# Head of a hybrid attention layer: fewer unused products, the second token tile normalised before a copy, and the conditioning rows before its transposes

## The chip, the cores and the metric

The kernel runs on one core of a Trainium2 chip. The metric is the device time of one execution in microseconds, the median over several runs. The engines are TensorE (PE in the profile; PEld its weight loads), VectorE (DVE), ScalarE (ACT), GpSimd (POOL) and SyncE (SP), whose queue issues nearly all loads. Each engine works through its own instructions in order; they wait for each other by semaphores.

## What is computed

One decoder layer in float32: 256 tokens, model width 1024. The part at the start is an adaptive norm, its result feeds one wide input projection, and behind that stand two attention branches, a gated merge and an output projection:

```python
mod = silu(c) @ w_ada + b_ada                       # conditioning: shift, scale, gate
shift, scale, gate = split(mod, 3)
h = rms_norm(x, g_pre) * (1 + scale) + shift        # x: 256 x 1024
proj = h @ w_in                                     # q/kv latents, MoBA q, k, v, gates
...
x = x + gate * rms_norm(y, g_post)
```

`rms_norm` multiplies each token by one over the root of the mean of its squares.

## The kernel before

Tokens lie in two tiles of 128 (`xs[0]`, `xs[1]`). The input comes in two loads: the first tile together with small constants (line 98), then the second tile (line 99). For the projection each weight and each input is split into a rounded part and its remainder, and three products are summed.

The kernel has a head and then a loop. The **head** (lines 309 to 350) makes the transposed, normalised input `xnT`, 8 blocks of 128 columns by 256 tokens. For each tile t: ScalarE squares it and sums (`ss`, line 332); VectorE makes the mean, GpSimd raises it to the power -0.5 (line 337), VectorE scales the tile (`xn[t]`, line 339); TensorE transposes it in two groups of four blocks (`pre_tr(t, 0)` into a bank `acc`, `pre_tr(t, 1)` into a bank `sc`), and a copy brings each group from the bank to `xnT`. The copy is on ScalarE where t equals the group's number and on VectorE otherwise. `pre_tr` records the transposes when it is called and gives back a function that records the copy.

Beside that, the **conditioning**: `ada_rows(j)` has eight products of the conditioning vector (`scp`) with a block of weights that is loaded in two halves (`raw` from `in_wada_dram`); `ada_evac(j)` copies the result to `rws` on ScalarE, `ada_cols(j)` turns it into columns by two narrow products with ones, `ada_ab(j)` makes scale and shift (`ab`) on VectorE. With these ScalarE makes the modulated block `h` of `xnT` (`h_act`), and the first projection product can run.

`busy(n)` (line 316) records n products of a tile of ones with itself; nothing reads them. A float32 product leaves two records in the trace.

The **loop** (`tokens`, with the string `STEP`) runs over the 8 weight blocks: in each step TensorE does the block's products and the next block's conditioning, and ScalarE and VectorE split the next block's weights (`s` and `d`). Raw weights lie in a ring of five buffers; `release` frees one and `pump` issues the next load on the SyncE queue. The first loads are issued in the order of `LOADS`: conditioning block 0 in two halves, weight block 0 in two parts, conditioning 1, weights 1, conditioning 2, and so on.

The order of the work in head and loop is written by hand: `ordered(eng, ...)` makes an instruction follow the last one so recorded on its engine, so program order is engine order there. Only behind the loop does a scheduler set it.

Of the kernel before, what the change touches and what calls it, by code (L numbers as in the profile page):

```python
# [10 lines left out]
FT = mybir.dt.float32  # L11
# [3 lines left out]
OP = mybir.AluOpType  # L15
# [3 lines left out]
P = 128  # L19
D = 1024  # L20
# [42 lines left out]
def hybrid_layer_kernel(ctx: ExitStack, tc: tile.TileContext, x, head, cst, gpost, bgate,  # L63
# [4 lines left out]
    wk = ctx.enter_context(tc.tile_pool(name="wk", bufs=2))  # L68
# [4 lines left out]
    V = nc.vector  # L73
# [4 lines left out]
    def ordered(eng, f, *a, **k):  # L78

        if eng in last_ins:  # L80
            with tc.issue_after(last_ins[eng]):
                r = f(*a, **k)  # L82
        else:
            r = f(*a, **k)
        last_ins[eng] = r.ins
        return r

    def bank(tag):
        return ps.tile([P, 512], FT, name=tag)
# [3 lines left out]
    xs = (first[:, 0:D], first[:, D + HEAD:])  # L93
# [79 lines left out]
    def ada_rows(j):  # L173
        r = raws["ada", j].rearrange("p (k n) -> p k n", k=KT)
        assert got["ada", j] == 2048
        for k in range(KT):
            g = 32 * (k % 4)
            ordered("T", mm, bR[g:g + 32, ROW:ROW + 256], scp[:, k], r[:, k], start=(k < 4), stop=(k >= 4),
                    skip_group_check=True)
        release()  # L180

    def ada_evac(j):
        rws[j] = wk.tile([P, 256], FT, name="rws", tag="acc", bufs=2)
        ordered("A", act, rws[j], bR[:, ROW:ROW + 256], AF.Copy)

    def ada_cols(j):
        r = rws.pop(j)
        for i in range(2):
            ordered("T", mm, bR[:, COL + 8 * i + j:COL + 1 + 8 * i + j], r[:, i * P:(i + 1) * P], ones[:, 0:1],
                    start=False, stop=True, skip_group_check=True)  # L190

    def ada_ab(j):
        ab = hab[j] = wk.tile([P, 2], FT, name="ab", bufs=2)
        ordered("V", V.scalar_tensor_tensor, ab[:, 1:2], bR[:, COL + 8 + j:COL + 9 + j], bsc[:, j:j + 1],
                gpre[:, j:j + 1], op0=OP.add, op1=OP.mult)
        ordered("V", V.tensor_tensor, ab[:, 0:1], bR[:, COL + j:COL + 1 + j], bsh[:, j:j + 1], op=OP.add)
# [114 lines left out]
    rs = sb.tile([P, 2], FT, name="rs")  # L311
# [4 lines left out]
    def busy(n):  # L316

        for _ in range(n):
            ordered("T", mm, bV[0][:, :P], ones, ones, start=True, stop=True)

    def pre_tr(t, g):
        b = bank(("acc", "sc")[g])
        for i in range(4):
            c0 = (4 * g + i) * P
            ordered("T", nc.tensor.transpose, b[:, i * P:(i + 1) * P], xn[t][:, c0:c0 + P], ident)
        dst, src = xnT[:, 4 * g:4 * g + 4, t * P:(t + 1) * P], b.rearrange("p (k n) -> p k n", k=4)
        if t == g:
            return lambda: ordered("A", act, dst, src, AF.Copy)
        return lambda: ordered("V", V.tensor_copy, dst, src)
# [1 line left out]
    for t in range(2):  # L331
        ordered("A", act, scr, xs[t], AF.Square, accum_out=ss[:, t:t + 1])
    xn = {}
    busy(24)
    for t in range(2):
        ordered("V", V.tensor_scalar, rs[:, t:t + 1], ss[:, t:t + 1], 1.0 / D, EPS, op0=OP.mult, op1=OP.add)
        pw = G.tensor_tensor(rs[:, t:t + 1], rs[:, t:t + 1], mhalf[:, 0:1], op=OP.pow)
        xn[t] = wk.tile([P, D], FT, name="xn", tag="xn", bufs=2)
        ordered("V", V.tensor_scalar, xn[t], xs[t], rs[:, t:t + 1], None, op0=OP.mult)
        pre_tr(t, 0)()  # L340
        if t == 0:
            pre_tr(t, 1)()
            busy(3)
    ada_rows(0)
    ada_evac(0)
    last_xnT = pre_tr(1, 1)
    ada_cols(0)
    busy(5)
    ada_ab(0)
    ordered("V", V.tensor_copy, posf, small[:, 211:213].bitcast(I32))  # L350

# [617 lines left out]
```

## Time and profile before

| | |
|---|---|
| median of 3 runs | 236.52 us (235.81 to 237.11) |
| the profiled execution's own time | 236.74 us |
| its span, first to last instruction | 234.9 us |
| TensorE busy | 224.6 us (96%) |
| VectorE, ScalarE, GpSimd busy | 169.6, 134.6, 50.9 us |
| mean granted TensorE clock | 0.992 |
| read from memory | 45.73 MB |

The span is what the trace covers; 1.84 us of the execution's time lie around it. A group in the trace is named by engine, line, operation and the tiles that it writes and reads. Line 82 is that of `ordered`, so everything in the head and loop carries it; such groups are told apart by tiles: `pv<-ones` is an unused product, `acc<-cstt,xn` and `sc<-cstt,xn` are transposes, `tr<-raw,scp` the conditioning rows, `tr<-ones,rws` the column products, `acc<-w,h` projection products. A note in brackets gives the time that the engine stood idle before the group and what ended it.

### The profile page before, as it was taken

What the parts mean: (1) busy time and instruction counts of PE and PEld (TensorE: products, weight loads), DVE (VectorE), ACT (ScalarE), POOL (GpSimd) and SP (SyncE); (2) the same over time, 40 slices, a digit from 0 to 9 for tenths busy, and PEclk for the clock granted to TensorE, in tenths of its full rate; (3) what the DMA queues carried; (4) which work ended last, traced back from release to release, by engine and by line L of the source; (5) the groups of instructions that cost most, each with busy time, mean ns of one, the idle gap of its engine ahead of it and who ended that gap; (6) DMA issues with size and microseconds to landing.
All of it is one profiled execution on the core that took longest, in us unless ns stands there. A gap on an engine that the chain in (4) does not pass through costs nothing.

```text
span 234.9 us, 4365 instructions
## 1 busy us (share of the span) xinstructions
PE 224.6 (96%) x1598; PEld 193.7 (82%) x1598; DVE 169.6 (72%) x418; ACT 134.6 (57%) x320; POOL 50.9 (22%) x81
## 2 busy tenths in 40 slices
PE   8789999999899999999999999999999999999990
PEld 8756666666699999999979988989998899998890
DVE  1354455444799767989979998999987466899543
ACT  4244444555866478649766996557477343564410
POOL 1138888600045101500000000000400000463000
PEclk9999999999999999999999999999999999999996
DMA  6999878998985534250550405788689720000022
GB/s 235 363 416 338 285 269 297 295 339 275 339 303 199 205 160 181 89 180 3 180 179 5 179 17 229 290 287 314 247 332 405 289 105 0 1 3 0 0 89 89
DMA packets 10247, 47.05 MB, mean 200 GB/s; under 512 B 1137, under 2 KB 1649, under 8 KB 7154
## 3 DMA queue, kind: packets, MB, share of 16 engines
q1 hardware_dynamic: 10226, 46.78, 54.4%
q8 instruction: 12, 0.20, 0.3%
q14 instruction: 9, 0.07, 0.1%
HBM read 45.73 MB, written 1.05 MB: 199 GB/s over the span
## 4 chain that ended last, share of the span: by engine, by line
PE 90%; DVE 3%; issue 2%; ACT 2%; POOL 1%; POOLq 0%; DVEq 0%; ACTq 0%
PE acc L436 9%; PE acc L438 9%; PE acc L437 9%; PE pv L82 8%; PE sc L82 6%; PE acc L82 6%; PE tr L82 5%; PE pv L705 3%; PE acc L764 3%; PE tr L695 2%; PE acc L765 2%; PE acc L766 2%; PE sc L672 2%; PE sc L664 2%; PE sc L888 2%
## 5 line engine op out<-in xcount | busy, mean ns | idle before, releaser
L266 ACT ACTIVATE w<-raw 128x512 fp32r<-128x512 f32 (+1 forms) x93 | 52.4, 617 | 34.3 <-PE acc L437 11.1
L266 DVE TENSOR_TENSOR w<-raw,w 128x512 fp32r<-128x512 f32 (+1 forms) x93 | 63.9, 727 | 6.2 <-ACT w L266 5.3
L436 PE MATMUL acc<-h,w 128*128 128x256 f32 x184 | 53.0, 288 | 0.1
L438 PE MATMUL acc<-h,w 128*128 128x256 f32 x184 | 52.8, 287 | 0.0
L437 PE MATMUL acc<-h,w 128*128 128x256 f32 x184 | 52.3, 284 | 0.0
L436 PEld LDWEIGHTS acc<-h,w 128*128 128x128 f32 x184 | 34.7, 188 | 1.2 <-issue 0.7
L438 PEld LDWEIGHTS acc<-h,w 128*128 128x128 f32 x184 | 34.7, 188 | 0.6
L437 PEld LDWEIGHTS acc<-h,w 128*128 128x128 f32 x184 | 34.7, 188 | 0.3
L82 DVE TENSOR_TENSOR w<-raw,w 128x512 fp32r<-128x512 f32 x24 | 17.0, 731 | 13.7 <-ACT w L82 13.2
L82 PE MATMUL sc<-w,h 128*128 128x512 f32 x48 | 16.6, 427 | 0.8 <-ACT xnT L82 0.5
L736 POOL TENSOR_TENSOR gacc<-gacc,bgt 1x1024 f32<-1x1024 f32 x1 | 2.6, 2580 | 67.7 <-PE acc L437 67.7
L776 POOL TENSOR_TENSOR y<-yy,y 128x256 fp32r<-128x256 f32 x8 | 8.5, 1073 | 37.3 <-ACT y L775 37.3
L82 PE MATMUL pv<-w,h 128*128 128x512 f32 x48 | 15.4, 406 | 1.0 <-ACT w L82 1.0
L82 PE MATMUL acc<-w,h 128*128 128x512 f32 x48 | 15.6, 410 | 0.0
L684 ACT ACTIVATE p<-p,mx 128x128 f32<-128x128 f32 (+1 forms) x32 | 14.2, 446 | 0.1
L82 ACT ACTIVATE w<-raw 128x512 fp32r<-128x512 f32 x23 | 13.5, 618 | 0.0
L82 ACT ACTIVATE rws<-tr 128x256 f32<-128x256 f32 x8 | 3.1, 385 | 16.9 <-PE tr L82 16.9
L82 PEld LDWEIGHTS sc<-w,h 128*128 128x128 f32 x48 | 8.0, 189 | 5.2 <-issue 2.9
L82 PEld LDWEIGHTS pv<-w,h 128*128 128x128 f32 x48 | 8.5, 188 | 4.3 <-ACT w L82 2.9
L82 PEld LDWEIGHTS acc<-w,h 128*128 128x128 f32 x48 | 8.5, 188 | 4.1 <-ACT h L82 2.5
L462 POOL TENSOR_TENSOR rr<-rr,m 128x512 f32<-128x512 f32 x4 | 5.6, 1420 | 25.5 <-DVE m L461 25.5
L697 ACT ACTIVATE pT<-tr 128x384 f32<-128x384 f32 x16 | 7.7, 487 | 5.7 <-PE tr L695 5.6
(255 smaller groups left out, 535.8 us busy)
## 6 DMA issues: line engine op xcount, KB each, us to landing
raw<-in_win_dram SPq DMA_DIRECT2D x12, 1024.0 KB, 4.8
raw<-in_wada_dram SPq DMA_DIRECT2D x16, 512.0 KB, 5.5
raw<-in_win_dram SPq DMA_DIRECT2D x8, 512.0 KB, 5.7
raw<-in_wadag_dram SPq DMA_DIRECT2D x4, 1024.0 KB, 4.7
raw<-in_wo_dram SPq DMA_DIRECT2D x4, 1024.0 KB, 5.2
raw<-in_wout_dram SPq DMA_DIRECT2D x4, 1024.0 KB, 9.4
raw<-in_win_dram SPq DMA_DIRECT2D x8, 256.0 KB, 5.9
raw<-in_winl_dram SPq DMA_DIRECT2D x2, 832.0 KB, 5.5
```

The source lines that it names most:

```text
L82: r = f(*a, **k)
L266: free = lambda eng, f, *a, **k: f(*a, **k)
L436: mm(o, w1[:, k], h1[:, k], start=(k == 0), stop=False)
L437: mm(o, w1[:, k], h2[:, k], start=False, stop=False)
L438: mm(o, w2[:, k], h1[:, k], start=False, stop=(k == KT - 1))
L462: eng.tensor_tensor(dst, dst, m2, op=OP.add)
L664: mm(sct[i][:, 0:P], view(q0, i), view(k0, i), start=True, stop=True)
L684: act(p[:, a:e], p[:, a:e], AF.Exp, scale=scale, bias=mx[:, t:t + 1], accum_out=sm[:, t:t + 1])
L697: act(pT, b[:, :384], AF.Copy)
L705: mm(b[64 * i:64 * i + 64, 0:S], v[0][:, h * 64:h * 64 + 64], pTt[br, h][:, 0:S], start=True, stop=False, skip_group_check=True)
L764: mm(o, w1[:, k, c0:c0 + P], u1[br][:, k], start=(k == 0), stop=False)
L776: G.tensor_tensor(y2[:, m], yy, y1[:, m], op=OP.subtract)
```

## The change

The change is in the head alone:

```diff
     xn = {}
-    busy(24)
+    busy(18)
+
+    def normed(t):
+        xn[t] = wk.tile([P, D], FT, name="xn", tag="xn", bufs=2)
+        ordered("V", V.tensor_scalar, xn[t], xs[t], rs[:, t:t + 1], None, op0=OP.mult)
+
     for t in range(2):
         ordered("V", V.tensor_scalar, rs[:, t:t + 1], ss[:, t:t + 1], 1.0 / D, EPS, op0=OP.mult, op1=OP.add)
         pw = G.tensor_tensor(rs[:, t:t + 1], rs[:, t:t + 1], mhalf[:, 0:1], op=OP.pow)
-        xn[t] = wk.tile([P, D], FT, name="xn", tag="xn", bufs=2)
-        ordered("V", V.tensor_scalar, xn[t], xs[t], rs[:, t:t + 1], None, op0=OP.mult)
-        pre_tr(t, 0)()
         if t == 0:
-            pre_tr(t, 1)()
-            busy(3)
+            normed(t)
+    normed(1)
+    pre_tr(0, 0)()
+    pre_tr(0, 1)()
     ada_rows(0)
     ada_evac(0)
+    pre_tr(1, 0)()
     last_xnT = pre_tr(1, 1)
     ada_cols(0)
-    busy(5)
+    busy(4)
     ada_ab(0)
```

Twenty-four unused products become 18 at the start, three become none between the tiles, five become four at the end. On TensorE the order of the head changes as follows (`pv<-ones` are the unused products, the first of them stands ahead of the piece; x4 or x8 is the count):

```order
-L82 MATMUL pv<-ones 128x128 x23
+L82 MATMUL pv<-ones 128x128 x17
 L82 MATMUL acc<-cstt,xn 128x128 x4
 L82 MATMUL sc<-cstt,xn 128x128 x4
-L82 MATMUL pv<-ones 128x128 x3
+L82 MATMUL tr<-raw,scp 32x256 x8
 L82 MATMUL acc<-cstt,xn 128x128 x4
-L82 MATMUL tr<-raw,scp 32x256 x8
 L82 MATMUL sc<-cstt,xn 128x128 x4
 L82 MATMUL tr<-ones,rws 128x1 x2
-L82 MATMUL pv<-ones 128x128 x5
+L82 MATMUL pv<-ones 128x128 x4
```

The conditioning rows now stand between the two tiles' transposes, where the three unused products stood, and all eight transposes of the second tile come behind them.

On VectorE, in the head, from the scaling of the first tile on (`xnT<-sc` is the copy of the first tile's second four transposes):

```order
 L82 TENSOR_SCALAR xn<-xs,rs 128x1024
-L82 COPY xnT<-sc 128x4x128
 L82 TENSOR_SCALAR rs<-ss 128x1
 L82 TENSOR_SCALAR xn<-xs,rs 128x1024
+L82 COPY xnT<-sc 128x4x128
 L82 COPY xnT<-acc 128x4x128
```

The second tile's mean and scaling move ahead of that copy. The order of ScalarE, GpSimd and the SyncE queue is the same as before, and so is every engine's order from the first projection product on.

## Rows read from the trace of the kernel before

**Rows 1.** Waits of PE over the whole span: total us, times, longest.
```profile
PE pv L82 <- ACT w L82: 1.0, 1, 1.0
PE sc L82 <- ACT xnT L82: 0.5, 1, 0.5
```

**Rows 2.** Timeline of PE in the head: start us, us, group, count.
```profile
7.48 1.50 PE L82 MATMUL pv<-ones 128*128 128x128 f32 x12
...
8.82 0.60 PE L82 MATMUL acc<-cstt,xn 128*128 128x128 f32 x4
9.69 0.83 PE L82 MATMUL pv<-ones 128*128 128x128 f32 x6
12.12 0.66 PE L82 MATMUL acc<-cstt,xn 128*128 128x128 f32 x4 [1.59 <-DVE xn L82]
12.70 1.07 PE L82 MATMUL tr<-raw,scp 128*32 128x256 f32 x16
13.71 0.66 PE L82 MATMUL sc<-cstt,xn 128*128 128x128 f32 x4
14.28 0.61 PE L82 MATMUL tr<-ones,rws 128*128 128x1 f32 x4
14.74 1.36 PE L82 MATMUL pv<-ones 128*128 128x128 f32 x10
16.04 0.74 PE L82 MATMUL acc<-w,h 128*128 128x512 f32 x2
```

**Rows 3.** Timeline of DVE and ACT in the head.
```profile
6.25 0.76 DVE L82 TENSOR_SCALAR xn<-xs,rs 128x1024 f32<-128x1024 f32 x1 [0.16 <-POOL rs L337]
6.62 0.19 ACT L82 ACTIVATION_READ_ACCUMULATOR scr<-xs 128x1 f32 x1
9.89 0.69 DVE L82 COPY xnT<-sc 128x512 f32<-128x512 f32 x1 [2.89 <-PE sc L82]
10.50 0.14 DVE L82 TENSOR_SCALAR rs<-ss 128x1 f32<-128x1 f32 x1
11.31 0.75 DVE L82 TENSOR_SCALAR xn<-xs,rs 128x1024 f32<-128x1024 f32 x1 [0.67 <-POOL rs L337]
15.39 0.60 ACT L82 ACTIVATE h<-xnT,ab 128x256 fp32r<-128x256 f32 x1 [1.16 <-DVE posf L82]
```

**Rows 4.** Timeline of the SyncE queue: four load issues, start us and us.
```profile
2.09 0.43 SPq L116 DMA_DIRECT2D raw<-in_wada_dram  x1
4.54 0.75 SPq L116 DMA_DIRECT2D raw<-in_win_dram  x1
8.21 0.33 SPq L116 DMA_DIRECT2D raw<-in_wada_dram  x1
13.83 0.33 SPq L116 DMA_DIRECT2D raw<-in_win_dram  x1
```

**Rows 5.** DMA issues at 2.09 and 4.54 alone: KB, us to landing.
```profile
raw<-in_wada_dram SPq DMA_DIRECT2D x1, 512.0 KB, 7.4
raw<-in_win_dram SPq DMA_DIRECT2D x1, 512.0 KB, 10.7
```

**Rows 6.** Busy by stretch: PE, PEld, DVE, ACT, POOL, granted clock, DMA share, GB/s.
```profile
0.98:6.03 5.05, 5.05 (x24) 5.05 (x25) 1.15 (x8) 2.64 (x5) 0.85 (x3) 1.00 0.82 286
...
228.00:230.00 2.00, 1.10 (x10) 0.89 (x8) 0.30 (x2) 0.48 (x2) 0.06 (x1) 1.00 0.47 174
230.00:232.00 2.00, 0.00 (x0) 0.00 (x0) 1.67 (x4) 0.00 (x0) 0.49 (x1) 0.82 0.00 1
```

**Rows 7.** Busy by stretch: the head's end, and one step of the loop.
```profile
12.12:16.04 3.92, 3.92 (x38) 2.89 (x39) 1.69 (x6) 1.04 (x3) 0.57 (x2) 1.00 1.03 417
19.40:25.55 6.15, 6.15 (x39) 4.01 (x38) 2.64 (x6) 3.04 (x6) 5.04 (x14) 1.00 0.87 305
```

**Rows 8.** Timeline of ACT in the first step: a weight split, the next evacuation.
```profile
17.91 0.62 ACT L82 ACTIVATE w<-raw 128x512 fp32r<-128x512 f32 x1
20.54 0.38 ACT L82 ACTIVATE rws<-tr 128x256 f32<-128x256 f32 x1 [2.02 <-PE tr L82]
```

## The prediction

> **What bounds the kernel now.** I read the waits of TensorE first. Over the whole span its longest waits behind the head are 1.0 us and 0.5 us [rows 1]; the scheduler kept the same order on every engine from the first product of the input projection on, so the change can act only on the head, the stretch before that product. The question is therefore how much earlier the product that starts at 16.04 us [rows 2] can start, and whether the rest moves with it.
>
> The timeline of TensorE in the head comes next. A product of ones with ones leaves two records, so the 24 unused products are 48. The last twelve of them fill 7.48 to 8.82 us, 0.11 us apart; then eight transposes of the first token tile take 0.87 us (8.82 to 9.69), then come three unused products (six records), and then TensorE stands still for 1.59 us until the normalised second tile is there, at 12.12 [rows 2]. The conditioning rows (12.70 to 13.71, 1.01 us), the last four transposes, the column products at 14.28 and the first real product at 16.04 follow.
>
> Third, the timeline of the other engines says why the second tile is late. The first tile is ready at 7.01 (6.25 + 0.76), and the second tile's sum of squares at 6.81, but VectorE's next instruction is the copy of the second four transposes, which starts at 9.89 after waiting 2.9 us for TensorE. Only behind it come the mean (10.50), the power on GpSimd and the scaling (11.31, ends 12.06) [rows 3]. So the second tile waits for a copy that does not concern it, and that copy waits for the transposes, and they for unused products.
>
> Last, the loads. The first half of the first conditioning weights had landed when the queue issued its next load at 8.21, which waits for the same semaphore; the second half was issued at 2.09 and landed 7.4 us later, at 9.49 [rows 4, 5]. Before, both were in long before 12.70. Now they matter.
>
> **The change, part by part.** *Six unused products fewer at the start.* They are the twelve records of the row from 7.48 on: the transposes of the first tile start at 7.48 in place of 8.82, 1.34 us sooner. The first tile is ready at 7.01 [rows 3], so it does not hold them up. At 0.87 us they are through at 8.35.
>
> [...]
>
> *The second tile's mean, power and scaling ahead of the copy.* From mean to finished tile they take 1.57 us (10.50 to 12.07) [rows 3]. They may now start at about 7.05, behind the first tile's scaling, so the second tile is ready at 8.6. The copy moves behind them, to about 8.6; it ends near 9.3, and its rows of the transposed input belong to weight blocks 4 to 7, used many steps later. Price: nothing.
>
> *Conditioning rows ahead of the second tile's transposes.* TensorE takes its queue in order. The rows' first eight records (half of 1.01 us) run from 8.35 to 8.85. The second eight wait for the load that lands at 9.49: a new wait of 0.64 us with the second tile's eight transposes, ready at 8.6, queued behind it. Rows done at 10.0. Transposes of the second tile, 0.87 us: to 10.87. ScalarE's evacuation of the rows takes until the column products 0.57 us (from the rows' end at 13.71 to 14.28) [rows 2]: 10.0 + 0.57 = 10.57, under the transposes. The column products start at 10.9 in place of 14.28.
>
> *Three unused products between the tiles gone, five at the end now four.* The three stood beside a wait, and go with it. The end of the head, 14.28 to 16.04, is set by the column products, two small VectorE operations and ScalarE's first activation (15.39 to 15.99) [rows 3]; the ten filler records from 14.74 on only fill [rows 2]. Four products end sooner by 0.22 us and change nothing. The first product: 10.9 + 1.76 = 12.7 us, so **3.35 us sooner**.
>
> *Does the rest follow?* One step of the projection loop takes 6.15 us with TensorE busy throughout, and the DMA engines at 0.87 of their time [rows 7]. Up to 16 us they run at 1.03, 417 GB/s [rows 7], so loads do not come sooner. The tightest two: the first half of the second weight block, issued at 4.54, lands 10.7 us later at 15.24 [rows 4, 5]; ScalarE splits it at 17.91 now, at 14.56 after a shift of 3.35, so it waits 0.7 us. But ScalarE stands still for 2.02 us behind this split, until the next evacuation at 20.54 [rows 8], and TensorE needs the split block only a step later. The same half of the third block: up to it three loads of 512 KB and one of 256 KB follow in the queue, 1.84 MB, at 417 GB/s 4.4 us, so it lands at about 19.7 (an estimate from these rows); its split comes a step after 17.91, at 24.1 now and 20.7 afterwards. One microsecond to spare. A step's loads are 1.84 MB too, 4.4 us against 6.15, so from there on the loads gain on the steps. I cost the rest at nothing; without this cover each late microsecond beyond the 2.02 would come off the gain. On the SyncE queue, the first load of the third weight block waits for the rows to free its buffer (issued 13.83 now [rows 4]); it can go at about 10.8, and joins a full queue behind loads issued before it.
>
> The sum, against the profiled execution: 236.74 - 3.35 = 233.4 us, span 231.5. It stands 0.22 us above the median of the three runs, 236.52, so the median should come to **233.2 us**.
>
> **Bounds of the unknown.** The new wait on a load is not in the trace of before. If the second half lands by 8.85, the wait is nothing and the gain 4.0 us. If it lands one half load later (0.52 MB at 417 GB/s, 1.26 us), the gain is 2.1 us. I take the landing of this trace, 9.49, since the loads ahead of it are issued as before.
>
> **Rivals.**
> *A. The loads take part of it back.* Either the second half lands late, or the splits of the next blocks do. For it: DMA at full rate until the first product, slack of only 1 us on the third block. Against: the queue's order up to it is unchanged, and a step asks for less than the engines bring. Price 1.26 us: 234.4 us. Chance 0.15.
> *B. The clock falls in the head (slower than before).* [...] Chance 0.06, a third of it with a short fall that ends near no change.
> *C. The shift is lost later.* Some later stage waits for something that does not move with the head. For it: nothing in the waits [rows 1]. Against: after the first blocks every load is issued upon a buffer's release, which moves too. 236.5 us, chance 0.06.
> *D. It goes as forecast*, 233.2 us with 232.3 to 234.0 around it for where the second half lands and the runs' scatter: 0.73.
>
> **How the numbers follow.** About 0.5% (1.2 us) is what a measurement of this kernel can tell from no change. D and A are faster by more: 0.88. C and a third of B: 0.08 the same. The rest of B: 0.04 slower. For 8 in 10 I need D and half of A: from the gain of 4.0 us less the scatter of the three runs (235.81 to 237.11), 232.1, to A's 234.4 with the same scatter, 235.0.
>
> **What would show it.** TensorE's first transposes at 7.5, no wait for the second tile, a wait on the conditioning load of about 0.6 us inside the rows, column products at 10.9, the first real product near 12.7; VectorE's second scaling finished by 8.7 with the copy behind it; ScalarE waiting for the second weight block's load, TensorE not; steps of 6.15 us as before. Wrong if the records in the head are 0.21 us apart, if the rows end after 11.3, or if the first product comes at 12.7 and the span still is over 233.

## The result, and the profile after

The changed kernel takes 233.51 us (median of 4 runs, 233.18 to 233.66) against 236.34 us for the kernel before beside it (4 runs, 235.81 to 237.11): 2.83 us less, ratio 0.9876 with a 95% interval of 0.9846 to 0.9906. It was forecast at 233.2 us, between 232.1 and 235.0. The profiled execution has a span of 231.4 us (forecast 231.5).

TensorE's timeline in the head of the changed kernel, the same view as [rows 2]:

```profile
1.57 6.27 PE L82 MATMUL pv<-ones 128*128 128x128 f32 x34
7.67 0.60 PE L82 MATMUL acc<-cstt,xn 128*128 128x128 f32 x4
8.11 0.60 PE L82 MATMUL sc<-cstt,xn 128*128 128x128 f32 x4
8.64 1.21 PE L82 MATMUL tr<-raw,scp 128*32 128x256 f32 x16
9.78 0.66 PE L82 MATMUL acc<-cstt,xn 128*128 128x128 f32 x4
10.27 0.60 PE L82 MATMUL sc<-cstt,xn 128*128 128x128 f32 x4
10.71 0.50 PE L82 MATMUL tr<-ones,rws 128*128 128x1 f32 x4
11.08 1.14 PE L82 MATMUL pv<-ones 128*128 128x128 f32 x8
12.37 0.73 PE L82 MATMUL acc<-w,h 128*128 128x512 f32 x2 [0.15 <-ACT h L82]
```

The stand of 1.59 us ahead of the second tile's transposes is gone; column products come at 10.71 in place of 14.28, the first projection product at 12.37 in place of 16.04: 3.67 us sooner. The sixteen conditioning records start 1.14 us ahead of what follows them (8.64 to 9.78) where it was 1.01 before: the new wait for the second half of the load is 0.13 us here.

VectorE's timeline answers to [rows 3]: the second tile's mean follows the first tile's scaling at once, and the copy that used to stand ahead of it comes behind the second scaling.

```profile
6.14 0.75 DVE L82 TENSOR_SCALAR xn<-xs,rs 128x1024 f32<-128x1024 f32 x1 [0.16 <-POOL rs L342]
6.88 0.15 DVE L82 TENSOR_SCALAR rs<-ss 128x1 f32<-128x1 f32 x1
7.70 0.76 DVE L82 TENSOR_SCALAR xn<-xs,rs 128x1024 f32<-128x1024 f32 x1 [0.67 <-POOL rs L342]
8.74 0.69 DVE L82 COPY xnT<-sc 128x512 f32<-128x512 f32 x1 [0.29 <-PE sc L82]
```

ScalarE's first step answers to [rows 8]. Here the shift does meet the loads: the split of the second weight block stands 1.35 us for its load. But the next evacuation still finds ScalarE idle for 0.57 us before it, so TensorE notices nothing.

```profile
15.67 0.63 ACT L82 ACTIVATE w<-raw 128x512 fp32r<-128x512 f32 x1 [1.35 <-DMA raw<-in_win_dram]
...
16.87 0.38 ACT L82 ACTIVATE rws<-tr 128x256 f32<-128x256 f32 x1 [0.57 <-PE tr L82]
```

The busy times by stretch for the same step of the loop as in [rows 7] (span, PE, PEld, DVE, ACT, POOL, clock, DMA share, GB/s):

```profile
15.73:21.88 6.15, 6.15 (x39) 4.01 (x39) 3.08 (x7) 3.73 (x7) 5.05 (x14) 1.00 1.03 411
```

The step still takes 6.15 us with TensorE busy throughout, and the DMA engines, at 0.87 of their time before, are full: 1.03 in this step and the next, 0.92 in the one after. The split of the third block's first half, at 20.95, stands 0.25 us for its load, which landed at 20.9 (issued at 10.51, 10.4 us); the next evacuation covers this too, with 1.50 us of idle time before it. From there the shift runs through; TensorE's last record starts at 228.82 us before and at 225.29 now, 3.53 us sooner, and the span is 3.5 us shorter.

### The profile page after: what moved, and what is told of

Read it like the earlier page. It is cut to its first block, busy times and chain, and to the rows that moved or that the text cites. A ratio compares the mean times of both kernels' runs of the same rounds, so it can differ in the third digit from the quotient of the medians.

```text
span 231.4 us, 4325 instructions
## 1 busy us (share of the span) xinstructions
PE 222.5 (96%) x1578; PEld 191.6 (83%) x1578; DVE 169.4 (73%) x418; ACT 134.3 (58%) x320; POOL 50.8 (22%) x81
## 4 chain that ended last, share of the span: by engine, by line
PE 91%; DVE 2%; issue 2%; ACT 2%; POOL 0%; POOLq 0%; DVEq 0%; ACTq 0%
PE acc L441 9%; PE acc L443 9%; PE acc L442 9%; PE pv L82 8%; PE sc L82 6%; PE acc L82 6%; PE tr L82 5%; PE pv L710 3%; PE acc L769 3%; PE tr L700 3%; PE acc L770 2%; PE acc L771 2%; PE sc L677 2%; PE sc L669 2%; PE sc L893 2%
## 5 line engine op out<-in xcount | busy, mean ns | idle before, releaser
L693 DVE TENSOR_SCALAR p<-p,sm 128x128 f32<-128x128 f32 (+1 forms) x32 | 10.8, 380 | 0.1
L82 ACT ACTIVATE h<-xnT,ab 128x256 fp32r<-128x256 f32 x8 | 4.8, 601 | 10.3 <-DVE ab L82 8.8
```

Source lines behind the costliest of these rows:

```text
L693: V.tensor_scalar(p[:, a:e], p[:, a:e], sm[:, t:t + 1], None, op0=OP.mult)
```

## The experiments

Nine other kernels ran, and the changed kernel once more. Each run lists its own times of the kernel before from the same chip; those medians were 236.22, 236.34 and 236.33 us in the three sets.

**VectorE's order alone**

```diff
     for t in range(2):
         ...
-        xn[t] = wk.tile(...)
-        ordered("V", ..., xn[t], ...)
-        pre_tr(t, 0)()
         if t == 0:
-            pre_tr(t, 1)()
-            busy(3)
+            normed(t)
+    normed(1)
+    pre_tr(0, 0)()
+    pre_tr(0, 1)()
+    busy(3)
+    pre_tr(1, 0)()
     ada_rows(0)
```

> The kernel before with one part of the change: the second tile's mean, power and scaling ahead of the copy on VectorE; all unused products and TensorE's order as before. My account: the 1.59 us stand of TensorE before the second tile goes, since that tile is ready at about 8.6 us; transposes of it start when the three unused products end, at about 10.4 in place of 12.12, the first projection product at about 14.3, and the time falls by 1.75 us (ratio 0.9926). Rival: the gain of the change is the unused products alone and the stand moves to something else; then no change. If the parts simply add, this one and the filler alone (the next run) make the whole.

Measured: 234.75 us (234.03 to 235.23), ratio 0.9931 (0.9907 to 0.9955). TensorE's timeline:

```profile
9.62 0.83 PE L82 MATMUL pv<-ones 128*128 128x128 f32 x6
10.29 0.60 PE L82 MATMUL acc<-cstt,xn 128*128 128x128 f32 x4
...
14.16 0.74 PE L82 MATMUL acc<-w,h 128*128 128x512 f32 x2
```

No wait stands ahead of the second tile's transposes, and the first product is at 14.16 (expected 14.3). By the medians about half of the whole gain, 1.5 of 2.8 us, comes from this order alone; the single times are spread over 1.2 us.

**Unused products alone**

```diff
-    busy(24)
+    busy(18)
...
-            busy(3)
...
-    busy(5)
+    busy(4)
```

> The kernel before with only the unused products of the change (18, 0 and 4 in place of 24, 3 and 5), all orders as before. My account: the transposes of the first tile start 1.1 to 1.3 us sooner and with them the copy, the mean, the scaling; the second tile's transposes start at about 10.8 to 11.0, the stand of TensorE before them grows to some 2.4 us, the first product comes at 14.7 to 14.9, and the time falls by 1.2 us (ratio 0.995). Rival, the clock: with a longer stand and no filler the records behind it lie 0.21 us apart and the time rises by up to 2 us.

Measured: 235.91 us (235.17 to 236.55), ratio 0.9988 (0.9968 to 1.0008): no gain that can be told from none. TensorE's timeline, then the busy times by stretch:

```profile
10.42 0.71 PE L82 MATMUL acc<-cstt,xn 128*128 128x128 f32 x4 [2.27 <-DVE xn L82]
11.06 1.94 PE L82 MATMUL tr<-raw,scp 128*32 128x256 f32 x16
12.93 1.12 PE L82 MATMUL sc<-cstt,xn 128*128 128x128 f32 x4
...
15.72 0.72 PE L82 MATMUL acc<-w,h 128*128 128x512 f32 x2 [0.16 <-ACT h L82]
```

```profile
9.30:10.42 1.12, 0.00 (x1) 0.01 (x1) 0.75 (x1) 0.00 (x0) 0.27 (x1) 1.00 1.03 406
10.42:11.06 0.64, 0.64 (x4) 0.41 (x5) 0.00 (x0) 0.00 (x0) 0.00 (x0) 0.86 0.99 336
11.06:12.00 0.94, 0.94 (x13) 0.48 (x16) 0.69 (x1) 0.00 (x0) 0.00 (x0) 0.50 1.02 336
```

The second tile does start sooner (10.42 against 12.12), but now the clock falls: after the unused products TensorE did eight transposes, stood 2.27 us, and within the next four transposes the granted clock goes from 1.00 to 0.50 (0.86 over these four). The sixteen conditioning records take 1.94 us in place of 1.07. The first product is at 15.72, 1 us later than expected with the level of 1.00 held. The ten times lie in two groups, five at 235.17 to 235.48 with a mean clock of 0.994 to 0.995 and five at 236.34 to 236.55 with 0.982 to 0.989; the profiled execution is one of the second group. So the median of 235.91 stands for neither: where the level holds, the removal brings 0.9 us, and where it falls, nothing.

**The same with the three products between the tiles kept**

```diff
-    busy(24)
+    busy(18)
...
-    busy(5)
+    busy(4)
```

> As the filler-only run (orders of before; 18 unused products at the start, 4 at the end), with the three between the two tiles kept. In the filler-only run the granted clock read 0.50 from about 10.9 to 14.05 us, and its times fell into two groups, 235.2 to 235.5 and 236.3 to 236.6 us. My account: the three products between the tiles are what kept the level in the kernel before; with them the granted clock stays 1.00 through the head, the records of the conditioning rows take 1.0 us in all, the first projection product comes at 14.6 to 14.9, and all times lie near 235.3 us. Rival: the level falls because there are fewer products at the start; then 0.50 shows again in the head and the two groups are back.

Measured: 235.14 us (234.98 to 235.55, seven runs, one group), ratio 0.995 (0.9929 to 0.997). TensorE's timeline:

```profile
8.47 0.83 PE L82 MATMUL pv<-ones 128*128 128x128 f32 x6
10.90 0.66 PE L82 MATMUL acc<-cstt,xn 128*128 128x128 f32 x4 [1.59 <-DVE xn L82]
11.49 1.07 PE L82 MATMUL tr<-raw,scp 128*32 128x256 f32 x16
...
14.82 0.72 PE L82 MATMUL acc<-w,h 128*128 128x512 f32 x2 [0.16 <-ACT h L82]
```

The conditioning records are back at 1.07 us, and the granted clock read 1.00 all through the head. To judge by the mean clock, 0.993 to 0.998 in all seven, no run lost the level. So these three products held the level; with VectorE's old order they are not idle filling. They do two things at once, run in the gap and shorten the stand from 2.27 to 1.59 us, and these runs do not tell which of the two counts.

**The rows put back** (this edit, as all that follow, is made to the changed kernel)

```diff
-    ada_rows(0)
-    ada_evac(0)
     pre_tr(1, 0)()
+    ada_rows(0)
+    ada_evac(0)
     last_xnT = pre_tr(1, 1)
```

> The changed kernel with the conditioning rows put back behind the second tile's first four transposes. My account: the move of the rows earns nothing; the second tile is ready when the first tile's transposes end, the rows then start at 9.0 and find the load landed, their evacuation hides under the last four transposes; column products at about 10.6 (10.71 in the changed kernel), the same time within 0.2 us, that is 2.8 to 3.0 us under the kernel before. Rival: the move is what makes the evacuation of the rows free, and without it 0.5 us are lost.

Measured: 233.31 us (233.24 to 233.38), ratio 0.9879 (0.9859 to 0.9899), the changed kernel's time. TensorE stands 0.41 us for the second tile, and none for the load:

```profile
8.69 0.66 PE L82 MATMUL acc<-cstt,xn 128*128 128x128 f32 x4 [0.41 <-DVE xn L82]
9.27 1.07 PE L82 MATMUL tr<-raw,scp 128*32 128x256 f32 x16
```

One small wait replaces another. The move of the conditioning rows earns nothing here, as was expected.

**Both moves, unused products as before**

```diff
-    busy(18)
+    busy(24)
...
     pre_tr(0, 1)()
+    busy(3)
     ada_rows(0)
...
-    busy(4)
+    busy(5)
```

> The changed kernel with the unused products of before (24, 3 and 5), the three between the first tile's transposes and the conditioning rows. My account: first transposes at 8.8, three products to 10.4, rows to 11.4, second tile's transposes to 12.3, first product at about 14.0; 2.0 us under the kernel before, 1.5 us over the changed one. Against the first run it tells what the rows' move does without a load to wait for: 0.2 to 0.3 us. Rival: the orders alone bring the whole gain, 233.5 us.

Measured: 233.78 us (233.69 to 234.89), ratio 0.9911 (0.9883 to 0.9938). The profiled execution is the slowest of the four, with first transposes at 9.05 and the first product at 14.28, near what was expected of it; the other three runs took 1.1 us less, 0.4 under the expectation. Their heads have no trace. So the rival comes close by the medians: the orders alone bring 2.4 of the 2.8 us, and dropping the ten unused products is worth 0.3 us more by the medians, 1.4 against the profiled execution. Against the run with VectorE's order alone the lowest and the highest time are each 0.34 us lower, about what was expected of the rows' move without a load to wait for; the medians differ by 1.0 us, as the times of either run are spread over 1.2 us. A likely reason for this spread, argued and not shown: how long the first products take depends on when the spacing of their records falls from 0.21 to 0.11 us, and that differs from profile to profile (near 6.0 us in the kernel before, near 6.4 in the changed one; below).

**Six unused products at the start**

```diff
-    busy(18)
+    busy(6)
```

> The changed kernel with 6 unused products at the start in place of 18. They end at about 3.6 us, and TensorE stands still until the first tile is ready at 7.0. My account: the level is still the lower one there, transposes take 1.7 us in place of 0.87, rows 2.0, transposes 1.7, column products 0.9, the first projection product comes near 14.5 and the first ones behind it are slow too; 1.5 to 4.5 us over the changed kernel, 235 to 238 us. Rival: the products at the start only fill; then 233.5 us or a little under, since transposes can start at 7.0.

Measured: 234.65 us (233.73 to 234.84), ratio 0.9919 (0.9887 to 0.9951), about 1.1 us over the changed kernel and less than expected; two of the five times are at 233.7 to 233.8, three at 234.7 to 234.8. TensorE's timeline:

```profile
7.01 1.12 PE L82 MATMUL acc<-cstt,xn 128*128 128x128 f32 x4 [3.11 <-DVE xn L82]
7.92 1.06 PE L82 MATMUL sc<-cstt,xn 128*128 128x128 f32 x4
8.91 1.67 PE L82 MATMUL tr<-raw,scp 128*32 128x256 f32 x16
10.51 0.66 PE L82 MATMUL acc<-cstt,xn 128*128 128x128 f32 x4
```

The eight transposes take 1.90 us (7.01 to 8.91) in place of 0.87, near the 1.7 expected: they lie 0.24 us apart, where the first 24 records of the kernel before lie 0.21 us apart [rows 6], and the granted clock reads 1.00 in both stretches. But the spacing falls during the conditioning rows, with no unused product near: the sixteen records take 1.60 us (1.01 before), and the next four transposes 0.50 us, to 11.01, which is 0.12 us each. This profiled execution took 233.79 us, so it is one of the two short ones, 0.3 us over the changed kernel's median; the three longer ones have no trace. So the twelve products at the start are worth 0.3 us in some executions and 1.1 in others, not 1.5 to 4.5.

**The second half of the conditioning load later**

```diff
-LOADS = "a00 a01 w00 w01 a10 a11 " + ...
+LOADS = "a00 w00 a01 w01 a10 a11 " + ...
```

> The changed kernel with the second half of the first conditioning weights loaded behind the first 512 KB of projection weights instead of ahead of them. My account: that half lands 1.26 us later, at 10.5 to 10.8 us; the rows' second half waits for it, with the second tile's transposes behind it; column products at 11.9, first projection product at 13.5, 1.1 us over the changed kernel: 234.6 us. Rival: the rows have slack and the time stays 233.5 us.

Measured: 235.49 us (234.6 to 236.56, ten runs), ratio 0.9959 (0.994 to 0.9978), 2.0 us over the changed kernel. TensorE's timeline and one stretch:

```profile
8.59 0.64 PE L82 MATMUL tr<-raw,scp 128*32 128x256 f32 x8 [0.34 <-DMA raw<-in_wada_dram]
11.07 0.64 PE L82 MATMUL tr<-raw,scp 128*32 128x256 f32 x8 [1.84 <-DMA raw<-in_wada_dram]
11.64 0.94 PE L82 MATMUL acc<-cstt,xn 128*128 128x128 f32 x4
```

```profile
12.00:13.00 1.00, 1.00 (x6) 1.00 (x5) 0.39 (x1) 0.16 (x1) 0.00 (x0) 0.50 0.99 381
```

The wait for the load is on the path, 1.84 us of it, and a second loss follows in this profile: the granted clock falls to 0.50 (0.94 from 11 to 12 us, 0.50 from 12 to 15). The mean clock was 0.985 to 0.989 in six of the ten runs and 0.996 to 0.998 in four; the medians of the two are 235.7 and 235.0 us, so by these medians the wait costs some 1.5 us and the fall another 0.7.

**The rows in two halves around the second tile's first transposes**

```diff
...
-    ada_rows(0)
+    ada_rows(0, range(4))
+    pre_tr(1, 0)()
+    ada_rows(0, range(4, 8))
     ada_evac(0)
-    pre_tr(1, 0)()
```

(`ada_rows` is given the range of products to record, and frees its buffer behind the last of them.)

> The changed kernel with the eight conditioning products cut in two: four ahead of the second tile's first transposes, four behind them. My account: the second tile is ready at 8.5, so its first four transposes run while the second half of the load arrives; the rows end at about 9.8, their evacuation hides under the last four transposes, column products at 10.3 in place of 10.7 to 10.9, first projection product near 12.0: 0.4 us under the changed kernel, 233.1 us (ratio 0.986). Rival: the load, not the order, sets the rows' end, and the time is that of the changed kernel.

Measured: 233.32 us (233.18 to 233.63), ratio 0.9868 (0.984 to 0.9895): the changed kernel's time. Two lines of TensorE and one of ScalarE:

```profile
8.41 0.64 PE L82 MATMUL tr<-raw,scp 128*32 128x256 f32 x8 [0.20 <-DMA raw<-in_wada_dram]
...
9.58 0.64 PE L82 MATMUL tr<-raw,scp 128*32 128x256 f32 x8
...
10.28 0.39 ACT L82 ACTIVATE rws<-tr 128x256 f32<-128x256 f32 x1 [1.88 <-PE tr L82]
```

The rival's time came, but not for its reason. The second half started at 9.58, straight behind the four transposes, and its load had landed just before, at 9.49 (issued at 2.09, 7.4 us): the trace shows no wait for it. TensorE waited 0.20 us for the first half instead, and the rows ended at 10.15, not 9.8. Only four transposes were left behind them, and ScalarE's evacuation, to 10.67, put the column products at 10.72, where the changed kernel has them at 10.71. What the division saves at the load it pays in these two places.

**No unused products at the end**

```diff
     ada_cols(0)
-    busy(4)
     ada_ab(0)
```

> The changed kernel without the four unused products at the end of the head. My account: they stand beside the chain from the column products through VectorE and ScalarE to the first projection product and set nothing; first product 1.7 us behind the column products as before, granted clock 1.00 throughout, 233.3 to 233.6 us. Rival: they hold the clock's level; then 0.50 shows in the first products and the time is 0.5 to 1.5 us longer, in some runs or all.

Measured: 234.08 us (233.52 to 234.91), ratio 0.99 (0.9869 to 0.9931). In the profiled execution nothing is lost (233.52, clock 1.00 in the head, TensorE standing 1.15 us ahead of the first product). In two of the four runs the mean clock is 0.986 and 0.987, and they take 234.38 and 234.91 us; the other two have 0.992 and 0.998. My account was right for the chain. For the clock it was wrong in two of four runs, to judge by their mean clock; where in them the level fell, no trace shows.

**The changed kernel again**, without an edit

> The changed kernel once more, for how steady it is. My account: it holds the clock's level in the head in every run, since TensorE never stands still there for more than the 0.1 to 0.7 us of the wait for the load; all times lie between 233.1 and 233.8 us, with no second group as in the filler-only run and the run with the late load. Rival: in some runs the load lands later and the level falls; then single times of 234.5 us and more.

Measured: 233.57 us (233.29 to 233.68, six runs), ratio 0.9872 (0.9848 to 0.9895); mean clock 0.993 to 0.999 in all. Its profile shows the spread of the head:

```profile
9.63 0.64 PE L82 MATMUL tr<-raw,scp 128*32 128x256 f32 x8 [0.24 <-DMA raw<-in_wada_dram]
...
12.78 0.72 PE L82 MATMUL acc<-w,h 128*128 128x512 f32 x2 [0.15 <-ACT h L82]
```

The first product is at 12.78 here and at 12.37 in the first profile, with waits for the load of 0.24 and 0.13 us.

No version beat the changed kernel clearly: with the rows back or in halves the medians are 0.2 us lower, within the intervals.

## Why the prediction was right

*The size.* 3.35 us were forecast and 2.83 measured between the medians. Between the two profiled executions it is 3.56 (236.74 to 233.18), but one of them lies 0.40 us above its median and the other 0.33 below. The changed kernel's second profile is nearer to its median: 233.67 us, 3.07 less, with the first product at 12.78 (forecast 12.7), 3.26 us sooner. So the sum for the head holds for the execution that it was made against. The step that fell short is the last, the carrying over of the 0.22 us by which that execution lay above the median: the scatter of the kernel before (235.81 to 237.11) is not the changed kernel's (233.18 to 233.66), so an offset from one does not hold for the other. The lower end of the range, 232.1, does not come out of its own terms: 236.52 less 4.0 and less the scatter on that side, 0.71, is 231.8. Nothing hung on it.

*The unused products at the start.* Forecast: transposes at 7.48. They came at 7.67, and in other profiles with 18 products between 7.06 and 7.78. That the spacing of the records falls from 0.21 to 0.11 us at 6.03 us [rows 6] was one execution's figure; in the changed kernel's profile it fell near 6.4. The term of 1.34 us for these products is therefore that execution's too: with both orders and all the products of before, three executions of four stand only 0.3 us over the changed kernel.

*VectorE's order.* Forecast: second tile ready at 8.6 and the stand of 1.59 us gone. It was ready at 8.46, and the order alone took 1.5 us off (expected 1.75).

*The rows ahead of the transposes.* Forecast: a new wait of 0.64 us, bounds 0 and 1.9. Measured 0.13 and 0.24, and 0.57 in the run without the end's products. The term was too large because TensorE arrived later and, in the first profile, the load sooner (7.1 us from issue at 2.09, not 7.4). That the move earns nothing was left unsaid; the run with the rows back shows it. The end of the head took 1.66 us (10.71 to 12.37), forecast 1.76.

*The rest follows.* The 3.67 us of the head's end are 3.53 at TensorE's last record. The second block's split waited 1.35 us (forecast 0.7), covered as argued. The third block's was to have one microsecond to spare and waited 0.25, since its load landed at 20.9 and not at 19.7; this was covered too.

*The clock.* Here the reasoning was too light, though the outcome held. I took the removal of the filler to cost nothing: an estimate of mine from one trace, where the conditioning rows' sixteen records took 1.07 us behind 1.59 us of standing [rows 2]. With the filler alone gone, and VectorE's order as before, the granted clock did fall to 0.50, and the same records took 1.94 us. The forecast came out because the two parts are in one change: the one takes away the stand that the other's products had guarded. Four kernels show it, by their mean clocks. With the stand and no products in it the level fell in five of ten runs (0.982 to 0.989); with the stand and three products in no run of seven (0.993 to 0.998); without the stand, with the products (VectorE's order alone) in none of five (0.994 to 0.997), and without either (the changed kernel) in none of ten (0.993 to 0.999). Apart the two parts bring 1.5 us and 0.3 us by the medians, together 2.8. The products at the end were also said only to fill, and without them two of four runs have the lower mean clock (0.986 and 0.987). So rival B, a fall of the clock in the head, came, but not in this kernel. With the unused products alone removed, five of ten runs had it as the short fall that ends near no change: some 1.1 us between the two groups, as the granted clock was back at 1.00 some 3 us after the fall, by 14.43 us, still in the head.

*Rival A* is the run with the late load: the price of 1.26 us was right in kind, and 2.0 us in fact, since TensorE waited longer than that, 1.84 us, and in six runs of ten the clock falls with it. None of the changed kernel's ten times shows that loss.

## What to carry to other kernels

Look for an instruction that stands in an in-order queue ahead of work it does not concern: one copy, waiting for another engine, kept the second tile back, and moving it was worth 1.5 us of the 2.8. Before taking out products that nobody reads, look at what TensorE does around them: where they stand next to a wait, take away the wait in the same step, and check the granted clock in more than one run: here, with a stand of 2.27 us left, the mean clock was lower in five runs of ten. Waits of 0.13 and 0.24 us for a load went with medians of 233.51 and 233.57 us; pushed back by one transfer, to 1.84 us, the wait cost 2.0 us.

## What the runs showed of the hardware that was not expected

The granted clock fell to 0.50 in the head in two profiles. Before the fall TensorE had done eight transposes and stood 2.27 us (unused products alone), or eight transposes, a stand of 0.34 us and eight conditioning records, and stood 1.84 us (late load). It held at 1.00 behind a stand of 1.59 us that came after eight transposes and three products (the kernel before, and the run with those kept). It is not the same in every run: six of ten late-load runs and five of ten with the unused products alone have a mean clock under 0.99, the others not.

The spacing of the records at the start changes too, at a granted clock of 1.00 throughout, and not always at the same time. In the kernel before the records came 0.11 us apart, after 0.21, from about 6.0 us on, in the changed kernel from about 6.4. In the run with the rows in halves all 18 products were through, and TensorE stood 0.40 us for the first tile:

```profile
7.12 0.66 PE L82 MATMUL acc<-cstt,xn 128*128 128x128 f32 x4 [0.40 <-DVE xn L82]
```

With 18 products TensorE waited for the tile there, and for the load in both profiles of the changed kernel (0.13 and 0.24 us). So one of these often sets the head's end, whenever the spacing falls, and the changed kernel's ten times lie within 0.5 us; those of the kernel before, with 24, lie within 1.3 us or more. That the spacing is the reason is argued from these profiles, not shown run by run.

In the changed kernel transposes and conditioning rows follow one another from 7.67 to 10.71, the transposes 0.11 to 0.12 us apart, and the granted clock reads 1.00. In the run with six products the spacing did not fall in 1.90 us of transposes, and it fell in the conditioning rows behind them; but in the kernel before, unused products too ran for 5.05 us before it fell [rows 6]. So whether transposes differ from products in this is not shown: no run here has transposes alone for longer.
